# The norm ahead of the feed-forward stages: two products with ones, a root and a reciprocal in place of column sums, a power and transposes

## The chip, the cores and the metric

The kernel runs on one core of a Trainium2 chip. The metric is device time in microseconds (us) of one execution, and lower is better. TensorE (PE) multiplies, VectorE (DVE) and ScalarE (ACT) do elementwise work, GpSimd (POOL) does a little of it, and SyncE (SP) issues most transfers. Each engine has one queue and takes its instructions in the order in which they stand in it.

## The reference

The program is a trunk of two layers over 512 tokens with 1024 features. Each layer mixes tokens by three branches and then runs a gated feed-forward stage with a causal convolution of width 3:

```
for l in range(DEPTH):
    h = rmsnorm(x, norm1_g[l])
    p = h @ w_in[l]
    ...
    x = x + jnp.sum(gates * proj, axis=2) @ w_out[l]
    x = x + conv_ffn(rmsnorm(x, norm2_g[l]), ffn_w_up[l], ffn_conv_w[l], ffn_conv_b[l], ffn_w_down[l])
return rmsnorm(x, final_g)
```

with `rmsnorm(x, g) = x * rsqrt(mean(x*x) + 1e-6) * g`, the mean over the 1024 features of a token. The change is in the second of these norms, `norm2`, once in each layer.

## The kernel before

**Layout.** Activations lie with features on the 128 partitions and tokens along the free axis, so x is eight tiles of 128x512 (names `x`, `xi`). The factor 1/rms of a token is the same for all features. The kernel therefore multiplies by the gain first (`norm_z`), starts the large products on x times gain, and multiplies their results by the token's factor afterwards. That factor, repeated on all 128 partitions, is the tile `rsF` (128x512).

**Exactness.** The products are split in three. Each float32 operand is parted into a rounded `hi` of type fp32r (a ScalarE cast) and a rest `lo` (a VectorE subtraction), and `mm3` issues hi*lo, hi*hi and lo*hi into one PSUM tile (line 153). A weight block of 128x512 comes in by a transfer (`wr`), is cast on ScalarE at line 136 and subtracted on VectorE at line 137. The halves are called `wh`/`wl` or `sh`/`sl`, by the pool that they lie in. One block feeds 12 products.

**The norm.** In `wout` the last eight products of the mixer give the new x. For each, `norm_sq` squares it on ScalarE (line 217) and VectorE adds it to a running tile (line 219), so that one 128x512 tile holds, by token, the sums over the eight blocks. What remains is the sum over the 128 partitions. `norm_stats` makes it by four float32 products with a column of ones, one for 128 tokens, which put the sums of a token on its own partition (128x4, line 229). VectorE scales them and adds epsilon (line 231), and GpSimd raises them to the power -0.5 (line 233, giving `rs`). `norm_rows` turns them back by four transposes of a broadcast column (line 238), and ScalarE copies the result out of PSUM into `rsF` (line 240).

**The feed-forward stage.** `ffn_up` makes 44 output columns of 24 products each. `firstF` runs the first three columns in halves: the first half of each (the four blocks of x that are ready first), and then the second halves. `norm_stats` stands before the fourth of these six steps and `norm_rows` before the fifth. Products that `firstF` issues keep their program order, the others are free to move. A column lies in one of four PSUM tiles `acc` and is released by VectorE's product `fu = acc * rsF` at line 1045. The fifth column takes the tile of the first. Behind `fu` come the convolution (`cv`, lines 1047 to 1049), a tanh on ScalarE (line 1053) and the gating.

**The order.** Apart from the pinned pieces, the order on each engine is set by a scheduler that simulates the program as it is built. An instruction without open inputs may be put anywhere from the place where its buffers are free. Other places that the prediction speaks of: line 456 issues and line 457 casts the small matrices `wua` at a mixer's start, line 472 makes the mixer's first columns `rwc`, line 483 is a tanh on one of them (`wax`), line 528 an exponential, line 960 a Gelu. Lines 970 are two products with the same 128x128 tile of ones in the spatial gating branch.

Of the kernel before, what the change touches and what calls it, by code (L numbers as in the profile page):

```python
# [10 lines left out]
AF = mybir.ActivationFunctionType  # L11
# [5 lines left out]
D = 1024  # L17
# [32 lines left out]
class Emit:  # L50
# [184 lines left out]
    def norm_rows(self):  # L235
# [3 lines left out]
        self.rsF = self.small((128, 512), "rsF", bufs=1)  # L239
        self.nc.scalar.copy(self.rsF, pb)  # L240

    def firstF(self, l, ids, st, at):


        self.h = st["z"]
        pss = [self.acc() for _ in ids]
        gs = [self.matFg(ps, ("wall", l, i, 0), self.h) for ps, i in zip(pss, ids)]
        self.pin = True
        for i, g in enumerate(gs + gs):
            if i == at[0]:  # L250
                self.norm_stats(st)
            if i == at[1]:
                self.norm_rows()
            next(g)
        self.pin = False
        return pss
# [742 lines left out]
    def wout(self, l, mg, xd, st):  # L999
        nc, V = self.nc, self.nc.vector  # L1000
        out = []
        for m in range(8):
            xi = self.u(n="xi")
            nc.sync.dma_start(xi, xd[m])
            ps = self.acc()
            self.matF(ps, ("wall", l, 70 + m, 0), mg)
            V.scalar_tensor_tensor(xi, ps, 0.5, xi, op0=MUL, op1=ADD)
            out.append(xi)
            self.norm_z(st, xi, "n2")
            self.norm_sq(st, xi)  # L1010
        return out
# [15 lines left out]
    def ffn_up(self, l, st, x):  # L1027
        nc, V, A = self.nc, self.nc.vector, self.nc.scalar
        nt = [0]

        def at():
            nt[0] += 1
            return (self.f if nt[0] <= NFP else self.r)(dt=F32R, n="ah")

        act = []
        first = self.firstF(l, (78, 79, 80), st, (3, 4))
        self.xt, turns = {}, [(c, g) for g in range(2) for c in range(NC)]
        for i in range(NFF):
            if l == L - 1 and i % 2 and turns:
                self.turn_x(x, *turns.pop(0))  # L1040
            cs = []
            for j in (i, NFF + i):
                ps = first.pop(0) if first else self.colF(l, 78 + 2 * i + (j >= NFF))
                u = self.u(n="fu")
                V.tensor_tensor(u, ps, self.rsF, op=MUL)  # L1045
                t = self.u(n="cv")
                A.activation(t, u, AF.Identity, scale=self.p("cw2", j), bias=self.p("cb", j))  # L1047
                V.scalar_tensor_tensor(t[:, 1:], u[:, :511], self.p("cw1", j), t[:, 1:], op0=MUL, op1=ADD)  # L1048
                V.scalar_tensor_tensor(t[:, 2:], u[:, :510], self.p("cw0", j), t[:, 2:], op0=MUL, op1=ADD)
                cs.append(t)  # L1050
            g, v = cs
            th = self.u(n="fth")
            A.activation(th, g, AF.Tanh, scale=0.5)
            V.scalar_tensor_tensor(th, th, 1.0, g, op0=ADD, op1=MUL)
            V.tensor_tensor(th, th, v, op=MUL)
            hi, lo = at(), at()
            A.copy(hi, th)
            V.tensor_tensor(lo, th, hi, op=SUB)
            act.append((hi, lo))
        return act  # L1060
# [210 lines left out]
```

## Time and profile before

| what | value |
|---|---|
| median of 3 runs | 1712.36 us (1712.04 to 1712.84) |
| the profiled execution: its time, its span | 1713.67 us, 1710.8 us |
| busy share of PE, DVE, ACT, POOL | 99%, 67%, 44%, 14% |
| granted TensorE clock | 1.000 |

The span runs from the first to the last instruction, and 2.9 us of the profiled execution lie outside it. A matmul of 128x512 is shown with about 0.39 us, but the next one starts before it ends, so that the starts tell the rate. A row of the timeline gives the start, the duration, the engine and the line, and in brackets the idle time before it and what ended that.

### The profile page before, as it was taken

The numbers are of one execution on the slowest core, as the hardware profiler recorded it, in microseconds if no ns is written. First come the engines' busy times: TensorE is split into PE (matmuls) and PEld (weight loads), VectorE is DVE, ScalarE is ACT, GpSimd is POOL, SyncE is SP. The second block draws the span as 40 slices with busy tenths as digits, with TensorE's granted clock in tenths as the row PEclk, the third lists the DMA queues.
The fourth block names the chain that finished last, engine by engine and source line by source line (L and its number), as shares of the span: only waits on it lengthen the run. The fifth ranks groups of instructions, "written<-read, shape, count | busy, mean of one in ns | idle before, by whom it ended". The sixth has DMA issues, their size and how long they took to land.

```text
span 1710.8 us, 27740 instructions
## 1 busy us (share of the span) xinstructions
PE 1700.5 (99%) x10328; PEld 1397.5 (82%) x10328; DVE 1149.7 (67%) x2056; ACT 750.4 (44%) x1258; POOL 247.0 (14%) x328
## 2 busy tenths in 40 slices
PE   9999999999999999999999999999999999999998
PEld 7888877888888888888888888777888888888887
DVE  7887756578568777653367786565775698886432
ACT  6564433534245444343256634345333454443322
POOL 1122235113200000000012203431131000000010
PEclk9999999999999999999999999999999999999999
DMA  5234555535443333233332345555254454432431
GB/s 181 93 104 143 149 140 146 156 116 173 142 154 93 99 99 97 70 116 111 116 113 79 114 143 151 136 145 178 84 188 150 134 135 116 125 110 69 154 99 56
DMA packets 149222, 212.81 MB, mean 124 GB/s; under 512 B 48096, under 2 KB 55264, under 8 KB 149088
## 3 DMA queue, kind: packets, MB, share of 16 engines
q1 hardware_dynamic: 129552, 171.62, 33.5%
q0 software_dynamic: 9600, 21.77, 4.8%
q10 hardware_dynamic: 9936, 17.65, 3.1%
q8 instruction: 81, 1.33, 0.3%
q14 instruction: 53, 0.43, 0.1%
HBM read 182.14 MB, written 23.07 MB: 120 GB/s over the span
## 4 chain that ended last, share of the span: by engine, by line
PE 97%; DMA 1%; DVE 0%; POOL 0%; issue 0%; ACT 0%; SPq 0%; DVEq 0%; POOLq 0%
PE acc L153 86%; PE sm L153 4%; PE sm L634 2%; PE acc L273 1%; PE sm L873 1%; PE sm L548 1%; DMA ws<-sgw 1%; PE sm L978 0%; POOL rs L698 0%; DMA x<-xT 0%; PE sm L511 0%; PE sm L510 0%; PE sm L901 0%; PE sm L928 0%; DVE wl L137 0%
## 5 line engine op out<-in xcount | busy, mean ns | idle before, releaser
L153 PE MATMUL acc<-lo,sh 128*128 128x512 f32 x1108 | 432.2, 391 | 0.0
L153 PE MATMUL acc<-hi,sh 128*128 128x512 f32 x1108 | 431.8, 390 | 0.0
L153 PE MATMUL acc<-hi,sl 128*128 128x512 f32 x1108 | 430.4, 389 | 0.0
L136 ACT CAST sh<-wr 128x512 fp32r<-128x512 f32 (+1 forms) x385 | 236.2, 617 | 409.6 <-PE acc L153 296.4
L137 DVE TENSOR_TENSOR sl<-wr,sh 128x512 fp32r<-128x512 f32 (+1 forms) x385 | 264.6, 691 | 174.9 <-ACT sh L136 106.1
L153 PEld LDWEIGHTS acc<-lo,sh 128*128 128x128 f32 x1108 | 208.0, 188 | 43.7 <-issue 0.3
L153 PEld LDWEIGHTS acc<-hi,sl 128*128 128x128 f32 x1108 | 208.0, 188 | 43.6 <-issue 0.3
L153 PEld LDWEIGHTS acc<-hi,sh 128*128 128x128 f32 x1108 | 208.0, 188 | 43.0 <-issue 0.5
L153 PE MATMUL acc<-lo,wh 128*128 128x512 f32 x556 | 219.5, 395 | 0.0
L136 ACT CAST wh<-wr 128x512 fp32r<-128x512 f32 x194 | 120.5, 621 | 223.7 <-PE acc L153 207.7
L153 PE MATMUL acc<-hi,wl 128*128 128x512 f32 x556 | 217.0, 390 | 0.0
L153 PE MATMUL acc<-hi,wh 128*128 128x512 f32 x556 | 216.6, 390 | 0.0
L137 DVE TENSOR_TENSOR wl<-wr,wh 128x512 fp32r<-128x512 f32 x195 | 137.8, 707 | 104.4 <-ACT wh L136 102.9
L153 PEld LDWEIGHTS acc<-lo,wh 128*128 128x128 f32 x556 | 104.3, 188 | 22.7 <-issue 0.3
L153 PEld LDWEIGHTS acc<-hi,wl 128*128 128x128 f32 x556 | 104.4, 188 | 22.6 <-issue 0.7
L153 PEld LDWEIGHTS acc<-hi,wh 128*128 128x128 f32 x556 | 104.4, 188 | 20.9
L153 PE MATMUL acc<-ah,sh 128*128 128x512 f32 x352 | 108.3, 389 | 0.0
L1045 DVE TENSOR_TENSOR fu<-acc,rsF 128x512 f32<-128x512 f32 x88 | 60.7, 690 | 65.8 <-PE acc L153 65.7
L1047 ACT ACTIVATE cv<-fu,pc 128x512 f32<-128x512 f32 x88 | 71.8, 817 | 47.7 <-DVE fu L1045 44.9
L153 PE MATMUL acc<-wl,hi 128*128 128x512 f32 x192 | 78.3, 408 | 2.1 <-DVE wl L137 2.1
L1048 DVE SCALAR_TENSOR_TENSOR cv<-fu,pc,cv 128x511 f32<-128x511 f32 x88 | 65.7, 747 | 20.2 <-ACT cv L1047 20.1
L153 PEld LDWEIGHTS acc<-ah,sh 128*128 128x128 f32 x352 | 66.1, 188 | 13.6
(320 smaller groups left out, 2434.7 us busy)
## 6 DMA issues: line engine op xcount, KB each, us to landing
wr<-wall SPq DMA_DIRECT2D x480, 256.0 KB, 2.7
gd<-gth ACTq DMA_DIRECT2D x48, 256.0 KB, 2.7
gth<-gd POOLq DMA_DIRECT2D x48, 256.0 KB, 3.5
wr<-wdt SPq DMA_DIRECT2D x44, 256.0 KB, 2.7
wr<-wdn SPq DMA_DIRECT2D x40, 256.0 KB, 2.7
x<-xT SPq DMA_DIRECT2D x8, 256.0 KB, 3.9
tn<-ysq POOLq DMA_DIRECT2D x32, 64.0 KB, 3.6
tab<-rot ACTq DMA_DIRECT2D x8, 256.0 KB, 3.3
```

Source lines behind the costliest of these rows:

```text
L136: self.kept((high or self.nc.scalar.copy)(hi[:, :n], raw[:, :n]))
L137: self.kept(self.nc.vector.tensor_tensor(lo[:, :n], raw[:, :n], hi[:, :n], op=SUB))
L153: i = self.nc.tensor.matmul(*x, **y, **kw)
L273: po(self.nc.tensor.matmul(pss[j], w[:, j * 128:j * 128 + 128], x, start=k == n == 0, stop=k == 7 and n == 2))
L548: i = T.matmul(pK[hv[1 - h], j, :], bk[hv[h], c, 1, :], x[hv[h], c, :], start=True, stop=True)
L634: po(T.matmul(o, l, r, start=start, stop=True, skip_group_check=True))
L873: po(T.matmul(X[h][:, i, :], lhsT, rhs, start=new[h], stop=stop, skip_group_check=True))
L1045: V.tensor_tensor(u, ps, self.rsF, op=MUL)
L1047: A.activation(t, u, AF.Identity, scale=self.p("cw2", j), bias=self.p("cb", j))
L1048: V.scalar_tensor_tensor(t[:, 1:], u[:, :511], self.p("cw1", j), t[:, 1:], op0=MUL, op1=ADD)
```

## The change

In the feed-forward stages, and there alone, `norm_ones` takes the place of `norm_stats` and `norm_rows`. The running tile is split into `hi` and `lo`, two full products with the tile of ones add its partitions, and every partition holds the sums of all 512 tokens at once. ScalarE takes the root of sum/1024 + epsilon out of PSUM, and VectorE takes the reciprocal in place, in two halves of 256. `wout` gets a root of one column of ones in front, whose result nobody reads.

```diff
--- before.py
+++ after.py
@@ -239,6 +239,18 @@
         self.rsF = self.small((128, 512), "rsF", bufs=1)
         self.nc.scalar.copy(self.rsF, pb)
 
+    def norm_ones(self, st):
+
+        hi, lo = self.split(st["acc"])
+        pb = self.sm()
+        for i, x in enumerate((lo, hi)):
+            self.tc.keep_in_program_order(self.nc.tensor.matmul(pb, self.ones, x, start=i == 0, stop=i == 1))
+        self.rsF = self.small((128, 512), "rsF", bufs=1)
+        self.nc.scalar.activation(self.rsF, pb, AF.Sqrt, scale=1.0 / D, bias=self.c("eps"))
+        for i in range(2):
+            h = self.rsF[:, 256 * i:256 * i + 256]
+            self.nc.vector.reciprocal(h, h)
+
     def firstF(self, l, ids, st, at):
 
 
@@ -247,9 +259,11 @@
         gs = [self.matFg(ps, ("wall", l, i, 0), self.h) for ps, i in zip(pss, ids)]
         self.pin = True
         for i, g in enumerate(gs + gs):
-            if i == at[0]:
+            if len(at) == 1 and i == at[0]:
+                self.norm_ones(st)
+            elif i == at[0]:
                 self.norm_stats(st)
-            if i == at[1]:
+            elif i == at[-1]:
                 self.norm_rows()
             next(g)
         self.pin = False
@@ -999,6 +1013,7 @@
     def wout(self, l, mg, xd, st):
         nc, V = self.nc, self.nc.vector
         out = []
+        nc.scalar.activation(self.small((128, 1), "ms"), self.c("ones"), AF.Sqrt)
         for m in range(8):
             xi = self.u(n="xi")
             nc.sync.dma_start(xi, xd[m])
@@ -1033,7 +1048,7 @@
             return (self.f if nt[0] <= NFP else self.r)(dt=F32R, n="ah")
 
         act = []
-        first = self.firstF(l, (78, 79, 80), st, (3, 4))
+        first = self.firstF(l, (78, 79, 80), st, (3,))
         self.xt, turns = {}, [(c, g) for g in range(2) for c in range(NC)]
         for i in range(NFF):
             if l == L - 1 and i % 2 and turns:
```

Line numbers of the kernel after are higher by 14 behind `firstF` and by 15 behind the head of `wout`: line 1060 there is line 1045 here, 1062 is 1047, 1068 is 1053, 497 is 483, 486 is 472, 471 is 457.

**TensorE, start of the first layer's feed-forward stage.** `acc_1095` is the fourth column, the three before it are those of `firstF`. Before, the column sums:

```order
L153 MATMUL acc_1095_5534<-lo_1014_5187,sh_1076_5449 128x512
L153 MATMUL acc_1095_5534<-hi_1013_5186,sh_1076_5449 128x512
L229 MATMUL sm_1072_5438<-con_78,sq_1059_5378 128x1 x4
L153 MATMUL acc_1060_5381<-lo_1025_5234,sh_1064_5386 128x512
L153 MATMUL acc_1060_5381<-hi_1024_5233,sh_1064_5386 128x512
```

and, on TensorE 25 products later, the transposes:

```order
L153 MATMUL acc_1095_5534<-hi_1057_5374,sh_1081_5474 128x512
L153 MATMUL acc_1095_5534<-hi_1057_5374,sl_1082_5475 128x512
L238 MATMUL sm_1078_5465<-con_78,rs_1074_5445 128x128 x4
L153 MATMUL acc_1061_5382<-lo_1025_5234,sh_1067_5404 128x512
L153 MATMUL acc_1061_5382<-hi_1024_5233,sh_1067_5404 128x512
L153 MATMUL acc_1061_5382<-hi_1024_5233,sl_1068_5405 128x512
```

Now both are gone, and the two products stand six products of the fourth column later:

```order
L153 MATMUL acc_1095_5531<-hi_1025_5235,sl_1082_5472 128x512
L153 MATMUL acc_1095_5531<-lo_1037_5283,sh_1081_5471 128x512
L153 MATMUL acc_1095_5531<-hi_1036_5282,sh_1081_5471 128x512
L247 MATMUL sm_1075_5444<-lo_1074_5441,ones_81 128x512
L247 MATMUL sm_1075_5444<-hi_1073_5440,ones_81 128x512
L153 MATMUL acc_1061_5383<-lo_1026_5236,sh_1065_5388 128x512
L153 MATMUL acc_1061_5383<-hi_1025_5235,sh_1065_5388 128x512
L153 MATMUL acc_1061_5383<-hi_1025_5235,sl_1066_5389 128x512
```

The 36 products that are the second halves of the first three columns follow the two in one piece, then the last seven of the fourth column, and then the fifth (`acc_1107`). Nothing else on TensorE has moved in the two layers.

**ScalarE, the same place.** `sq` is the running tile. Before:

```order
L136 CAST sh_1097_5537<-wr_1080_5472 128x512
L136 CAST sh_1100_5555<-wr_1083_5490 128x512
L136 CAST sh_1109_5588<-wr_1096_5535 128x512
L136 CAST sh_1112_5606<-wr_1099_5553 128x512
L136 CAST sh_1118_5631<-wr_1108_5586 128x512
L240 COPY rsF_1079_5470<-sm_1078_5465 128x512
L1047 ACTIVATE cv_1087_5510<-fu_1086_5508,pc_45_181 128x512
L136 CAST sh_1121_5649<-wr_1111_5604 128x512
L1047 ACTIVATE cv_1089_5516<-fu_1088_5514,pc_45_181 128x512
L1053 ACTIVATE fth_1090_5520<-cv_1087_5510 128x512
```

Now:

```order
L145 CAST hi_1073_5440<-sq_1060_5380 128x512
L136 CAST sh_1100_5552<-wr_1083_5487 128x512
L136 CAST sh_1109_5585<-wr_1096_5532 128x512
L249 ACT_TABLE_LOAD
L249 ACTIVATE rsF_1076_5447<-sm_1075_5444,con_78 128x512
L136 CAST sh_1112_5603<-wr_1099_5550 128x512
L136 CAST sh_1118_5628<-wr_1108_5583 128x512
L1062 ACTIVATE cv_1087_5507<-fu_1086_5505,pc_45_181 128x512
L1062 ACTIVATE cv_1089_5513<-fu_1088_5511,pc_45_181 128x512
L136 CAST sh_1121_5646<-wr_1111_5601 128x512
L1068 ACT_TABLE_LOAD
L1068 ACTIVATE fth_1090_5517<-cv_1087_5507 128x512
```

The split stands between two weight casts, the root with a switch of the function table behind the cast `sh_1109`, and one more switch before the first tanh. VectorE has at the same place, before:

```order
L137 TENSOR_TENSOR sl_1101_5556<-wr_1083_5490,sh_1100_5555 128x512
L231 TENSOR_SCALAR ms_1073_5443<-sm_1072_5438 128x4
L137 TENSOR_TENSOR sl_1110_5589<-wr_1096_5535,sh_1109_5588 128x512
L137 TENSOR_TENSOR sl_1113_5607<-wr_1099_5553,sh_1112_5606 128x512
L137 TENSOR_TENSOR sl_1119_5632<-wr_1108_5586,sh_1118_5631 128x512
L1045 TENSOR_TENSOR fu_1086_5508<-acc_1060_5381,rsF_1079_5470 128x512
L1048 SCALAR_TENSOR_TENSOR cv_1087_5510<-fu_1086_5508,pc_45_181,cv_1087_5510 128x511
```

And now VectorE has:

```order
L146 TENSOR_TENSOR lo_1074_5441<-sq_1060_5380,hi_1073_5440 128x512
L137 TENSOR_TENSOR sl_1101_5553<-wr_1083_5487,sh_1100_5552 128x512
L137 TENSOR_TENSOR sl_1110_5586<-wr_1096_5532,sh_1109_5585 128x512
L252 RECIPROCAL rsF_1076_5447<-rsF_1076_5447 128x256 x2
L137 TENSOR_TENSOR sl_1113_5604<-wr_1099_5550,sh_1112_5603 128x512
L1060 TENSOR_TENSOR fu_1086_5505<-acc_1061_5383,rsF_1076_5447 128x512
L1060 TENSOR_TENSOR fu_1088_5511<-acc_1062_5384,rsF_1076_5447 128x512
L137 TENSOR_TENSOR sl_1119_5629<-wr_1108_5583,sh_1118_5628 128x512
L1063 SCALAR_TENSOR_TENSOR cv_1087_5507<-fu_1086_5505,pc_45_181,cv_1087_5507 128x511
```

The two reciprocals stand ahead of one weight subtraction and of the first `fu`.

**ScalarE, start of the first layer.** `wh` are weight casts for the mixer's columns. ScalarE's queue before:

```order
L456 DMA wua_68_234<-wua 128x512
L136 CAST wh_80_329<-wr_77_323 128x512
L457 CAST wus_69_235<-wua_68_234 128x512
L136 CAST wh_85_354<-wr_78_325 128x512
L240 COPY rsF_83_350<-sm_82_345 128x512
L472 ACTIVATE rwc_88_374<-rwp_87_372,omu_60_219 128x512
L472 ACTIVATE rwc_101_400<-rwp_100_398,omu_60_219 128x512
L136 CAST wh_108_416<-wr_79_327 128x512
L472 ACTIVATE rwc_103_405<-rwp_102_403,omu_60_219 128x512
L483 ACTIVATE wax_89_377<-rwc_88_374 64x512 x2
L472 ACTIVATE rwc_105_410<-rwp_104_408,omu_60_219 128x512
L519 ACTIVATE cs_146_562<-rwc_101_400,pc_45_181 128x512
```

Now:

```order
L136 CAST wh_80_329<-wr_77_323 128x512
L1016 ACT_TABLE_LOAD
L1016 ACTIVATE ms_972_5006<-con_78 128x1
L471 CAST wus_69_235<-wua_68_234 128x512
L136 CAST wh_85_354<-wr_78_325 128x512
L240 COPY rsF_83_350<-sm_82_345 128x512
L486 ACTIVATE rwc_88_374<-rwp_87_372,omu_60_219 128x512
L486 ACTIVATE rwc_101_400<-rwp_100_398,omu_60_219 128x512
L136 CAST wh_108_416<-wr_79_327 128x512
L486 ACTIVATE rwc_103_405<-rwp_102_403,omu_60_219 128x512
L497 ACT_TABLE_LOAD
L497 ACTIVATE wax_89_377<-rwc_88_374 64x512 x2
```

The root that is written at the head of `wout` has no inputs that come late, and the scheduler has put it at the layer's start, a whole mixer ahead of `wout`. Behind it the tanh needs a switch back. In the second layer it is the same, where the tanh's switch replaces one that stood at line 528 before. In all the program now has 12 table switches, and before it had 5.

## The prediction

> **What bounds the kernel now.** I read the first part of the page, then the chain that ended last, then the list of TensorE's waits.
>
> ```profile
> span 1710.8 us, 27740 instructions
> PE 1700.5 (99%) x10328; PEld 1397.5 (82%) x10328; DVE 1149.7 (67%) x2056; ACT 750.4 (44%) x1258; POOL 247.0 (14%) x328
> PE 97%; DMA 1%; DVE 0%; POOL 0%; issue 0%; ACT 0%; SPq 0%; DVEq 0%; POOLq 0%
> PE acc L153 <- DVE wl L137: 2.1, 2, 1.1
> PE acc L294 <- DVE rst L291: 1.5, 1, 1.5
> PE acc L273 <- ACT hi L211: 0.4, 1, 0.4
> ```
>
> TensorE is busy for 99% of the span, holds 97% of the chain, and waits for other engines for 2.1 + 1.5 + 0.4 = 4.0 us in all. Only the two waits of 1.1 us or less lie in the middle of the program. So the time is the number of TensorE's instructions by their rate, as long as the others keep up. Two questions follow: what TensorE's own work in the norm costs, and whether the added work on ScalarE and VectorE makes TensorE wait.
>
> **TensorE's part.** The rate comes from the starts in TensorE's timeline around the first layer's norm.
>
> ```profile
> 496.70 0.39 PE L153 MATMUL acc<-lo,sh 128*128 128x512 f32 x1
> ...
> 504.86 0.39 PE L153 MATMUL acc<-lo,sh 128*128 128x512 f32 x1
> 505.09 0.39 PE L153 MATMUL acc<-hi,sh 128*128 128x512 f32 x1
> 505.32 0.95 PE L229 MATMUL sm<-con,sq 128*128 128x1 f32 x8
> ...
> 511.71 0.39 PE L153 MATMUL acc<-hi,sl 128*128 128x512 f32 x1
> 511.93 0.60 PE L238 MATMUL sm<-con,rs 128*128 128x128 f32 x4
> ...
> 517.84 0.39 PE L153 MATMUL acc<-lo,sh 128*128 128x512 f32 x1
> ...
> 1354.27 0.39 PE L153 MATMUL acc<-hi,sh 128*128 128x512 f32 x1
> ...
> 1371.78 0.39 PE L153 MATMUL acc<-lo,sh 128*128 128x512 f32 x1
> ```
>
> From 496.70 to 504.86 there are 36 products by the program's order: 8.16 / 36 = 0.2267 us each. From 504.86 to 511.71 there are 26 with the sums between them: 6.85 - 26 x 0.2267 = 0.96 us for the sums. From 511.71 to 517.84 there are 25 with the transposes between: 6.13 - 25 x 0.2267 = 0.46 us. In the second layer 71 products lie between 1354.27 and 1371.78, with both pieces: 17.51 - 71 x 0.2267 = 1.41 us. So the removed work costs 1.42 and 1.41 us, somewhat less than the 0.95 + 0.60 us of the two rows, whose ends overlap the next product.
>
> The kernel before already has two products like the added ones, in the gating branch:
>
> ```profile
> L970 PE MATMUL sm<-lo,ones x2: 389/389/389, 350.8 to 1200.0; 128*128 128x512 f32 x2
> L970 PE MATMUL sm<-hi,ones x2: 389/389/389, 351.0 to 1200.2; 128*128 128x512 f32 x2
> ```
>
> They have the duration of the products of line 153 and start 0.2 us apart, so each costs 0.227 us: 0.45 us for two. The gain is 1.42 - 0.45 = 0.97 us in the first layer and 0.96 in the second, together 1.93 us. Its bounds: 0 if something else takes it back, 2.83 if the two products were free.
>
> **Is the split there in time?** Rows of VectorE (the last sum into the running tile) and ScalarE (weight casts) in the same stretch:
>
> ```profile
> 500.07 0.69 DVE L219 TENSOR_TENSOR sq<-sq,sq 128x512 f32<-128x512 f32 x1
> 500.12 0.62 ACT L136 CAST sh<-wr 128x512 fp32r<-128x512 f32 x1 [0.23 <-ACT sq L217]
> 502.84 0.62 ACT L136 CAST sh<-wr 128x512 fp32r<-128x512 f32 x1 [2.10 <-PE acc L153]
> 505.56 0.62 ACT L136 CAST sh<-wr 128x512 fp32r<-128x512 f32 x1 [2.10 <-PE acc L153]
> ```
>
> The running tile is complete at 500.76. The cast `hi` (0.62 like its neighbours) fits into the 2.10 us in which ScalarE waits, and `lo` (0.69) follows on VectorE: done at about 502.2. The first product with ones starts seven products after 505.09, at 506.68, 4.5 us later. The split costs nothing; its cover is ScalarE's idle time, and without it TensorE would have to wait only after 4.5 us.
>
> **Is rsF there in time?** This is the piece that could cost something. The products end near 506.90 + 0.39 = 507.29. Then come a table switch, the root and two reciprocals. From ScalarE's timeline at a Gelu, the groups of VectorE's instructions, and its timeline at the first `fu`:
>
> ```profile
> 329.02 0.63 ACT L136 CAST sh<-wr 128x512 fp32r<-128x512 f32 x1
> 329.67 1.28 ACT L960 ACT_TABLE_LOAD   x1
> 330.96 0.63 ACT L960 ACTIVATE sgu<-sgu 128x512 f32<-128x512 f32 x1
> L532 DVE RECIPROCAL F<-cs 128x7 f32<-128x7 f32 x8 | 1.6, 197 | 0.1
> L753 DVE RECIPROCAL TMP<-TMP 128x32 f32<-128x32 f32 x2 | 0.7, 348 | 0.0
> L679 DVE TENSOR_TENSOR S<-S,F 128x256 f32<-128x256 f32 x12 | 5.1, 424 | 0.3
> 513.21 0.68 DVE L1045 TENSOR_TENSOR fu<-acc,rsF 128x512 f32<-128x512 f32 x1
> ```
>
> A switch takes 1.28 us; the root about 0.6, like the other ScalarE passes over 128x512. No reciprocal of 256 columns is shown. The rows of 7 and 32 columns give (348 - 197) / 25 = 6.0 ns for a column, so 348 + 224 x 6.0 = 1.69 us for 256. [...] I take 1.69, from the operation itself. Then: 507.29 + 1.28 + 0.6 = 509.2; two reciprocals, 512.6; one weight subtraction ahead of `fu` in the queue, some 0.6, 513.2; `fu` done at 513.9, the same as before (513.21 + 0.68). The fifth column, which needs that tile, starts 45 products after 506.68, at 516.88 (before: 517.84). The margin is 3.0 us, so this costs nothing as well. The next `fu` follow 0.7 us apart, and each is needed only 24 products, 5.4 us, later. [...]
>
> [...]
>
> **The other switches.** Seven are added, 7 x 1.28 = 9.0 us on ScalarE, which is busy for 44%. Two of them per layer were costed or lie next to it: the root's, above, and the tanh's behind it, where the weight halves are made far ahead (the cast of 505.56 is `sh_1109`, which TensorE first reads 86 products behind the one of 505.09, some 20 us later). The unread root and the switch back lie at the layer's start, for which these are rows of the timelines:
>
> ```profile
> 26.41 0.62 ACT L457 CAST wus<-wua 128x512 fp32r<-128x512 f32 x1 [3.10 <-DMA wua<-wua]
> 31.97 1.26 ACT L483 ACTIVATE wax<-rwc 64x512 f32<-64x512 f32 x2
> 34.50 0.60 ACT L136 CAST wh<-wr 128x512 fp32r<-128x512 f32 x1
> 35.31 0.65 DVE L137 TENSOR_TENSOR wl<-wr,wh 128x512 fp32r<-128x512 f32 x1
> 37.19 0.73 ACT L472 ACTIVATE rwc<-rwp,omu 128x512 f32<-128x512 f32 x1 [1.04 <-DVE rwp L470]
> 38.45 0.39 PE L153 MATMUL acc<-hi,wl 128*128 128x512 f32 x1
> 867.15 0.62 ACT L136 CAST wh<-wr 128x512 fp32r<-128x512 f32 x1 [3.01 <-PE acc L153]
> ```
>
> The unread root (1.28 + about 0.3) falls into idle time of 3.10 us in the first layer and of 3.01 us in the second: nothing. The switch back stands before the tanh of 31.97 and moves the cast of 34.50 and the subtraction of 35.31 by 1.28 us; `wl` is then ready at 37.24, and TensorE first reads it at 38.45. The margin of 2.49 us falls to 1.2. ScalarE's idle 1.04 us at 37.19 takes up most of the delay. Cost nothing. In the second layer a switch at line 528 goes away in return.
>
> Taken out on other engines: line 231, line 233 on GpSimd and ScalarE's copy, none of which TensorE waits for. The sum for the profiled execution is 1713.67 - 1.93 = 1711.7 us. The median is 1.31 us lower than that execution, so 1712.36 - 1.93 = 1710.4 us.
>
> **Rivals.**
>
> *The gain is given back (1712.4).* If somewhere behind the norms another engine sets the pace, TensorE arrives there earlier and waits. For it: the two waits for `wl` show such places. Against: 4.0 us of waits in all, and what VectorE does there is itself released by TensorE's products. Both gains would be lost.
>
> *More is gained (1708.3).* If the two waits for `wl`, 2.1 us, also go because ScalarE and VectorE are loaded otherwise: 1710.4 - 2.1. For it: the second layer loses a switch at line 528 ahead of the second wait. Against: it gets one earlier in return, and the order there hasn't moved.
>
> [...]
>
> *A late start of the mixer (slower: 1715.9).* If the two ScalarE pieces at a layer's start (1.28 + 1.28 + 0.2) weren't absorbed and came back in full as waits for `wl` in each layer: 1710.4 + 2 x 2.76. Against: the idle rows just shown.
>
> That the change doesn't do what it says is excluded by the order: the products, root and reciprocals stand there.
>
> **How the numbers follow.** Chances: forecast 0.72, given back 0.11, more gained 0.06, rsF late 0.06, late mixer 0.05. The time is 1710.4. The forecast's own range is 1709.5 to 1711.3 (runs of before lie 0.8 apart). Up to 1713.2 the given-back case and part of a late rsF are in, down to 1709.0 a part of the larger gain: 1709.0 to 1713.2 holds some 0.85. A measurement of this kernel can tell about 0.2%, 3.4 us, from no change: below 1708.9 it is faster, above 1715.8 slower. The larger gain lies beyond the first bound, and half of the last rival beyond the second, with something for what I haven't seen: 0.06 faster, 0.89 same, 0.05 slower.
>
> **What would show it.** Right: two products at the new line 247 with 0.45 us between their neighbours, no wait of TensorE at 507 or for the fifth column's tile, `fu` near 513, twelve table loads of 1.28 us, and the weight subtraction of 35.31 up to 1.3 us later. Wrong: reciprocals above 3 us, a wait of TensorE behind `fu`, or waits for `wl` at a layer's start or longer ones than 1.1 us.

## The result, and the profile after

The changed kernel takes 1709.25 us (median of 15 runs, 1708.48 to 1710.52), beside 1712.36 us for the kernel before (15 runs, 1711.23 to 1713.84). The ratio is 0.9982, with a 95% interval from 0.9975 to 0.9989, so between 1.9 and 4.3 us are gained. The forecast was 1.93 us. The profiled execution took 1709.09 us, with a span of 1707.4 us.

From the page of the changed kernel, its span, busy times and the shares of the chain that ended last:

```profile
span 1707.4 us, 27709 instructions
PE 1697.3 (99%) x10308; PEld 1395.7 (82%) x10308; DVE 1156.7 (68%) x2060; ACT 758.1 (44%) x1269; POOL 244.2 (14%) x326
PE 98%; DMA 1%; DVE 0%; POOL 0%; issue 0%; ACT 0%; SPq 0%; DVEq 0%; POOLq 0%
```

And the list of TensorE's waits (total, times, longest, in us):

```profile
PE acc L153 <- DVE wl L137: 1.7, 2, 0.9
PE acc L308 <- DVE rst L305: 1.5, 1, 1.5
PE acc L287 <- DVE wh L136: 0.8, 1, 0.8
```

Nothing has changed in kind. TensorE is still busy for 99% and waits at the same three lines of the program, 4.0 us in all as before. It waits nowhere for `rsF` or `fu`. It has 20 instructions fewer: in each layer the sums had 8 and the transposes 4, and the products with ones are 2. With the reciprocals VectorE's busy time is higher by 7.0 us in all, and with the table loads ScalarE's by 7.7, beside TensorE's work.

TensorE's timeline of the changed kernel at the first layer's norm, and at the first product of the fifth column:

```profile
505.90 0.39 PE L153 MATMUL acc<-hi,sh 128*128 128x512 f32 x1
506.13 0.39 PE L247 MATMUL sm<-lo,ones 128*128 128x512 f32 x1
506.36 0.39 PE L247 MATMUL sm<-hi,ones 128*128 128x512 f32 x1
506.58 0.39 PE L153 MATMUL acc<-lo,sh 128*128 128x512 f32 x1
...
516.33 0.39 PE L153 MATMUL acc<-lo,sh 128*128 128x512 f32 x1
```

The two products with ones stand in the stream like any other: 506.58 - 506.13 = 0.45 us for both, and no idle time in brackets at any row, the fifth column's included. Now the chain from the sums to `fu`, first ScalarE's timeline, then VectorE's:

```profile
500.15 0.62 ACT L145 CAST hi<-sq 128x512 fp32r<-128x512 f32 x1
...
505.66 1.28 ACT L249 ACT_TABLE_LOAD   x1
506.95 0.69 ACT L249 ACTIVATE rsF<-sm,con 128x512 f32<-128x512 f32 x1
```

```profile
500.84 0.68 DVE L146 TENSOR_TENSOR lo<-sq,hi 128x512 fp32r<-128x512 f32 x1
...
507.67 3.37 DVE L252 RECIPROCAL rsF<-rsF 128x256 f32<-128x256 f32 x2 [1.31 <-ACT rsF L249]
510.95 0.63 DVE L137 TENSOR_TENSOR sl<-wr,sh 128x512 fp32r<-128x512 f32 x1
511.50 1.42 DVE L1060 TENSOR_TENSOR fu<-acc,rsF 128x512 f32<-128x512 f32 x2
```

The split is done at 501.52, and its first reader starts at 506.13. The table load begins at 505.66, while TensorE still makes the sums, and ends at 506.94, 0.2 us behind the last of them (506.36 + 0.39). So it is all but out of the chain. The row of 511.50 holds two `fu`; the first ends near 512.2, and the fifth column needs it at 516.33. The margin is 4.1 us.

### The profile page after: what moved, and what is told of

It reads as the page before. It is cut to its first block, busy times and chain, and to the rows that moved or that the text cites. A ratio compares the mean times of both kernels' runs of the same rounds, so it can differ in the third digit from the quotient of the medians.

```text
span 1707.4 us, 27709 instructions
## 1 busy us (share of the span) xinstructions
PE 1697.3 (99%) x10308; PEld 1395.7 (82%) x10308; DVE 1156.7 (68%) x2060; ACT 758.1 (44%) x1269; POOL 244.2 (14%) x326
## 4 chain that ended last, share of the span: by engine, by line
PE 98%; DMA 1%; DVE 0%; POOL 0%; issue 0%; ACT 0%; SPq 0%; DVEq 0%; POOLq 0%
PE acc L153 87%; PE sm L153 4%; PE sm L648 2%; PE acc L287 1%; PE sm L887 1%; PE sm L562 1%; DMA ws<-sgw 1%; PE sm L992 0%; POOL rs L712 0%; DMA g<-pcols 0%; PE sm L525 0%; PE sm L524 0%; PE sm L915 0%; PE sm L942 0%; PE sm L800 0%
```

## The experiments

**Where the time went.** Four points of TensorE's timeline part the program into stretches that hold one thing each: the gating branch's products with ones in both layers, the first sums of the second layer's `norm1`, and the last product. The rows of the kernel before, and of the changed one:

```profile
350.81 0.39 PE L970 MATMUL sm<-lo,ones 128*128 128x512 f32 x1
...
863.50 0.95 PE L229 MATMUL sm<-con,sq 128*128 128x1 f32 x8
...
1199.99 0.39 PE L970 MATMUL sm<-lo,ones 128*128 128x512 f32 x1
...
1704.29 0.40 PE L153 MATMUL acc<-sh,ah 128*128 128x256 f32 x2
```

```profile
350.26 0.39 PE L984 MATMUL sm<-lo,ones 128*128 128x512 f32 x1
...
861.77 0.95 PE L229 MATMUL sm<-con,sq 128*128 128x1 f32 x8
...
1197.58 0.39 PE L984 MATMUL sm<-lo,ones 128*128 128x512 f32 x1
...
1700.91 0.40 PE L153 MATMUL acc<-sh,ah 128*128 128x256 f32 x2
```

Stretch A runs to the first point and C from the second to the third: each holds a mixer and no changed norm. B lies between them, and D runs from the third point to the end of the last product: each holds one changed norm and its feed-forward stage. The starts give, for all kernels of the study (us):

| kernel | A | B | C | D |
|---|---|---|---|---|
| before | 350.81 | 512.69 | 336.49 | 504.70 |
| before, another execution | 350.07 | 512.68 | 336.35 | 504.70 |
| before, with the unread root | 350.04 | 512.47 | 335.81 | 504.71 |
| changed | 350.26 | 511.51 | 335.81 | 503.73 |
| changed, another execution | 350.75 | 511.51 | 335.27 | 503.74 |
| changed, without the unread root | 350.24 | 511.51 | 336.36 | 503.74 |
| both norms | 351.03 | 512.93 | 336.53 | 505.16 |
| ten times the products | 349.92 | 515.62 | 336.15 | 507.82 |
| three times the reciprocals | 350.02 | 517.41 | 336.06 | 509.58 |
| `ws` first | 349.07 | 511.51 | 334.64 | 503.74 |

In two executions of one kernel B and D repeat to 0.01 us; A and C scatter by a microsecond, whichever norm the kernel has. That makes two questions. Do B and D fall by what TensorE's instructions cost, or by another cause (the switches, a change in how the engines meet)? And what makes A and C scatter, which the gain beyond 1.93 us must come from?

**The same kernel again**, timed beside the next two on one chip.

> The changed kernel once more. Theory P (TensorE's own work alone): two stages of 0.97 us less, so 1.93 us below the kernel before, a ratio of 0.9989; what came out beyond it, 3.1 - 1.9 = 1.2 us, is scatter between executions, and the starts in a second trace differ from the first by up to about 1 us at places that have nothing to do with the norms. Rival S (the table switches also help the rest of the program): 3.1 us again, 0.9982, and the steps of the shift against the kernel before lie at the same places as in the first trace.

Measured: 1709.05 us (11 runs), with 1711.67 for the kernel before; the ratio is 0.9986, from 0.9977 to 0.9994. D differs from the kernel before by 504.70 - 503.74 = 0.96 us, and B by 1.18. The gain in the medians is 2.6 us here and 3.1 in the first comparison, and isn't better known than to about a microsecond.

> The kernel before once more, one look, for its trace: how far TensorE's starts differ between two executions of one kernel. Theory P: up to about 1 us over the span, gathered in small steps where TensorE runs many short products or waits for a weight half. Rival S: less than 0.3 us, so that 1.4 us of shift outside the norms must be an effect.

Measured: one execution of 1711.59 us, with a span of 1709.9. Its B and D are those of the first trace, its A is 0.74 us shorter, and so is TensorE's one wait for `wl` in that stretch, 0.23 us by 0.97.

**Switches, one way and the other.** First the changed kernel without the unread root in `wout`, and so with 8 table loads in place of 12:

```diff
-        nc.scalar.activation(self.small((128, 1), "ms"), self.c("ones"), AF.Sqrt)
```

> The changed kernel without the unread root at the head of wout. On every engine the same instructions in the same order, but for eight ScalarE instructions less: two roots and two table loads in front of the mixers, two loads back (less one that returns at the exponential). Theory P: ScalarE's idle time hid them, so the time is that of the changed kernel within 0.3 us (ratio to the kernel before 0.9989). Rival S: the 1.2 us beyond the forecast came from the moved switches and go with them: 1.2 us slower than the changed kernel. Rival L (the late mixer of the prediction in small): the switches cost and the time falls by up to 2.8 us more.

Measured: 1709.44 us (11 runs), ratio 0.9987 from 0.9978 to 0.9996; B and D are as with the root to 0.01 us. Then the kernel before with that line added, and so with 8 table loads in place of 5:

> The kernel before with the unread root alone; the sums, the power and the transposes stay. Eight table loads in place of five. Theory P: 1.0000, the kernel before within 0.3 us, and the weight subtraction of 35.31 is 1.3 us later with TensorE's starts unmoved. Rival S: 1.2 us faster, 0.9993. Rival L: slower by up to 5.5 us.

Measured: 1711.36 us (11 runs), ratio 0.9999 from 0.9990 to 1.0008. Whatever would put a gain or a loss down to the switches falls on both sides: the four further loads there and the three here cost nothing that can be measured, and bring nothing. The unread root in particular doesn't spare the load at the norm. The groups of ScalarE's instructions in the changed kernel show why:

```profile
L1016 ACT ACT_TABLE_LOAD x2 | 2.6, 1283 | 0.0
L497 ACT ACT_TABLE_LOAD x2 | 2.6, 1283 | 0.0
L974 ACT ACT_TABLE_LOAD x2 | 2.6, 1283 | 0.0
L249 ACT ACT_TABLE_LOAD x2 | 2.6, 1283 | 0.0
```

The root's set comes in at line 1016 at the layer's start, the tanh's at line 497 and the Gelu's at line 974 follow, and so the load at line 249 is still there, twice. What hides the pieces at a layer's start is seen in ScalarE's timeline:

```profile
23.39 1.28 ACT L1016 ACT_TABLE_LOAD   x1
24.68 0.20 ACT L1016 ACTIVATE ms<-con 128x1 f32<-128x1 f32 x1
26.43 0.62 ACT L471 CAST wus<-wua 128x512 fp32r<-128x512 f32 x1 [1.55 <-DMA wua<-wua]
...
32.10 1.28 ACT L497 ACT_TABLE_LOAD   x1
...
35.94 0.60 ACT L136 CAST wh<-wr 128x512 fp32r<-128x512 f32 x1
...
38.63 0.72 ACT L486 ACTIVATE rwc<-rwp,omu 128x512 f32<-128x512 f32 x1 [1.04 <-DVE rwp L484]
```

The first load and the root lie in the idle time before the cast of `wus`, of which 1.55 us are left from 3.10. The second moves the weight cast from 34.50 to 35.94, and TensorE doesn't wait for it.

**The removed work back in.** The changed kernel with the old sums, power and transposes at their old places beside the new norm. Their result isn't used, one column of it is copied and left (the edit in part):

```diff
+                self.norm_stats(st)
...
+            elif len(at) == 1 and i == at[0] + 1:
+                self.norm_rows(False)
```

> The changed kernel with the old column sums, the power and the four transposes of each feed-forward stage put back beside the new ones; of their result one column is copied and nobody reads it. Theory P: TensorE gets back what the prediction priced at 1.42 and 1.41 us, so the time is 2.8 us above the changed kernel: 1.6 us or so below 1713.6 on a scale on which the changed kernel stands at 1709.1, that is 1711.9, and level with the kernel before (ratio 1.000 to 1.001). In the trace the stretch from the first layer's norm to the next mixer's norm grows from 355.64 to 357.06 us, the one from the second norm to the end from 347.87 to 349.28. Rival D (what was saved were the durations of the records, 0.95 + 0.60): 3.1 us. Rival H (the sums were hidden): no change against the changed kernel, 0.9985.

Measured: 1712.51 us (11 runs), ratio to the kernel before 1.0003 from 0.9994 to 1.0012. B grows by 512.93 - 511.51 = 1.42 us and D by 505.16 - 503.74 = 1.42. That is the price that the prediction read from the spacing of starts (1.42 and 1.41), not that of the durations shown in the rows (0.95 + 0.60 = 1.55), and it isn't hidden.

**The added work ten times.** Each pair of products with ones is made ten times into the same tile:

```diff
-        for i, x in enumerate((lo, hi)):
-            self.tc.keep_in_program_order(self.nc.tensor.matmul(pb, self.ones, x, start=i == 0, stop=i == 1))
+        for i, x in enumerate((lo, hi) * 10):
+            self.tc.keep_in_program_order(self.nc.tensor.matmul(pb, self.ones, x, start=i % 2 == 0, stop=i % 2 == 1))
```

> The changed kernel with the two products with ones issued ten times in each stage, the last pair being used: 18 more products in each, the order on the other engines the same. Theory P: 18 x 0.2267 = 4.08 us in each stage, 8.16 us in all, 1717.3 where the changed kernel stands at 1709.1; one pair then costs 0.453 us. Rival: the products cost their whole duration of 0.39 us, 14.0 us in all; or nothing, if TensorE has slack there.

Measured: 1718.03 us (6 runs), ratio 1.0034 from 1.0022 to 1.0047. B is 4.11 us longer than in the changed kernel and D 4.08; 18 products by 0.2267 us are 4.08. With this, both sides of TensorE's sum are measured: 1.42 out, 0.45 in.

**The reciprocals late.** Each half is inverted three times, which gives the same value, and 6.9 us more on VectorE ahead of `fu`:

```diff
-        for i in range(2):
+        for i in (0, 1) * 3:
```

> The changed kernel with the reciprocals taken three times over (the reciprocal of the reciprocal of the reciprocal, so the value is the same): four more of 256 columns in each stage, 4 x 1.66 = 6.6 us more on VectorE ahead of the first product with rsF, with three weight subtractions between and behind them, where the changed kernel has one. In the trace of the changed kernel that product ends at 512.2, and the fifth column needs its tile at 516.3: a margin of 4.2 us. Theory P (rsF costs nothing until the fifth column needs the tile, and one for one from there): about 6.6 + 1.2 + some 0.6 of waiting for the casts = 8.4 us later, less 4.2, so TensorE stands for about 4.2 us in each stage, 8.5 us in all: 1717.6. By the margin of 3.0 us of the prediction it would be 2.4 us more. Rival H: VectorE's queue is covered further on too, and the time stays at 1709.1.

Measured: 1721.24 us (5 runs), ratio 1.0055 from 1.0043 to 1.0068. The pause came about as reckoned, and something else with it. TensorE's waits for `fu` in the list of its waits, and then its timeline around the first one:

```profile
PE acc L153 <- DVE fu L1060: 7.9, 2, 4.0
```

```profile
515.86 0.39 PE L153 MATMUL acc<-hi,sl 128*128 128x512 f32 x1
520.21 0.50 PE L153 MATMUL acc<-lo,sh 128*128 128x512 f32 x1 [3.96 <-DVE fu L1060]
...
521.03 0.62 PE L153 MATMUL acc<-lo,sh 128*128 128x512 f32 x1
521.45 0.63 PE L153 MATMUL acc<-hi,sh 128*128 128x512 f32 x1
...
524.43 0.40 PE L153 MATMUL acc<-hi,sl 128*128 128x512 f32 x1
524.67 0.39 PE L153 MATMUL acc<-lo,sh 128*128 128x512 f32 x1
```

Behind the pause of 3.96 us the products start 0.42 us apart for 3.4 us, from 521.03 to 524.43, instead of 0.23. B is longer than in the changed kernel by 5.90 us and D by 5.85, so each layer pays 1.9 us beyond the pause. The windows of the same kernel name it (the stretch and its length, the busy times of the five engines with their instructions, TensorE's granted clock, the DMA engines' share and GB/s):

```profile
520.20:524.50 4.30, 4.29 (x12) 3.38 (x13) 3.93 (x6) 2.78 (x3) 0.00 (x0) 0.60 0.32 116
524.50:529.00 4.50, 4.50 (x21) 3.70 (x20) 3.81 (x7) 3.72 (x7) 0.00 (x0) 1.00 0.05 8
```

The clock is 0.60 in the mean of the first window and 1.00 behind it. To tell whether the extra goes with the length of the pause (theory P) or is a fixed price from some length on (theory G), three kernels make it shorter and longer, by further reciprocals that leave the values as they are. The edit of the shortest is shown; the second has 192 in place of 128, and the longest has `(0, 1, 0, 1, 0, 1, 0, 0)` in the first loop and not the second one:

```diff
-        for i in range(2):
+        for i in (0, 1, 0, 0):
...
+        for w in (128, 128):
+            self.nc.vector.reciprocal(self.rsF[:, 0:w], self.rsF[:, 0:w])
```

> The changed kernel with two further reciprocals over 256 columns and two over 128 (the first half is inverted five times, the second once, so the values are the same). With 1.72 us for 256 columns and 0.87 for 128, and the stall of 3.96 us that four further ones of 256 columns made, TensorE's pause behind fu should be 3.96 - 2 x 1.72 + 2 x 0.87 = 2.3 us in each layer. Theory G (a pause longer than some length between 1.1 and 4.0 us lowers the clock for a fixed time): either no product slower, and a span of 1707.4 + 2 x 2.3 = 1712.0, or the same extra of 1.9 us in each layer, 1715.8. [...] Rival P (the extra grows with the pause, 1.9 / 3.96 = 0.48 of it): products spaced wider for about 1.1 us in sum in each layer, a span of 1714.2.

> As the one with the pause of 2.3 us, with 192 columns in place of 128 (1.3 us each by the same rate): a pause of 3.96 - 2 x 1.72 + 2 x 1.3 = 3.1 us in each layer. Theory G: no product slower, a span of 1707.4 + 2 x 3.1 = 1713.6, or the same extra of 1.9 us in each layer, 1717.4, or the extra in one layer alone, if the length from which it acts is near 3 us. Rival P: an extra of 0.48 x 3.1 = 1.5 us in each layer, a span of 1716.6.

> The changed kernel with six further reciprocals of 256 columns (the first half five times, the second three times, the same values): a pause of 3.96 + 2 x 1.72 = 7.4 us in each layer. Theory G: the extra behind the pause is the same 1.9 us, a span of 1707.4 + 2 x (7.4 + 1.9) = 1726.0. Rival P: an extra of 3.5 us in each layer, 1729.2.

Measured, one execution each, beside 1712.3 us for the kernel before; B and D are given against the changed kernel's 511.51 and 503.73:

| kernel | time, span | pause | B | D | beyond the pause |
|---|---|---|---|---|---|
| two of 128 | 1717.32, 1715.6 | 2.84 | +4.77 | +3.14 | 1.93 and 0.30 |
| two of 192 | 1720.22, 1718.5 | 3.4 | +5.35 | +5.32 | 1.9 |
| three times | 1721.24, 1719.2 | 3.96 | +5.90 | +5.85 | 1.9 |
| six more | 1729.09, 1727.4 | 7.5 | +9.38 | +9.39 | 1.8 |

The pauses of the first two came out 0.3 to 0.5 us longer than expected, in part since 128 columns take 0.94 us and 192 take 1.34. Theory P falls: from 3.4 to 7.5 us the extra stays at 1.8 to 1.9. The first kernel holds the decisive pair, in TensorE's timeline, and in the windows behind its two pauses:

```profile
519.37 0.50 PE L153 MATMUL acc<-lo,sh 128*128 128x512 f32 x1 [2.84 <-DVE fu L1062]
...
1371.73 0.50 PE L153 MATMUL acc<-lo,sh 128*128 128x512 f32 x1 [2.84 <-DVE fu L1062]
```

```profile
519.37:523.40 4.03, 4.03 (x11) 3.21 (x12) 3.74 (x6) 1.50 (x2) 0.00 (x0) 0.59 0.09 33
1371.73:1376.00 4.27, 4.27 (x19) 3.53 (x20) 3.98 (x9) 2.75 (x3) 0.00 (x0) 1.00 0.09 33
```

The same pause in the same place lowers the clock in the first layer and not in the second, with the same share of the DMA engines (0.09) in both windows. So the slow spell isn't contention with transfers. The waits of up to 1.42 us that the kernels of the table have in their mixers don't bring it: behind the longest of them the products start 0.33 us apart once and then 0.23 to 0.24. Two narrower windows show where it lies in the first layer:

```profile
519.37:520.13 0.76, 0.76 (x3) 0.67 (x4) 0.54 (x1) 0.76 (x2) 0.00 (x0) 1.00 0.46 175
520.13:523.54 3.41, 3.41 (x9) 2.64 (x8) 3.34 (x5) 0.74 (x2) 0.00 (x0) 0.50 0.00 0
```

The clock is 1.00 for 0.76 us behind the pause and then 0.50 for 3.41 us, in which nothing is transferred. So the spell doesn't begin with the pause's end here, nor does it with three times the reciprocals, where the first wide spacing follows the start at 521.03, 0.82 us behind the pause. Behind the first pause of 7.5 us the spacing is wide from the first product on (starts at 525.08, 525.67 and 526.10). By the two pauses of 2.84 us it isn't the length of a pause alone that decides. What else does isn't shown: no run moved a pause to try it.

**What scatters in A and C.** In the mixers TensorE waits for `wl`, between 0.23 and 1.08 us in stretch A and between 0.29 and 1.42 in C in the nine rows of the table that have these waits. What is late there? From the timelines of the kernel before, TensorE's and then VectorE's:

```profile
307.84 0.39 PE L153 MATMUL acc<-wh,lo 128*128 128x512 f32 x1
309.20 0.50 PE L153 MATMUL acc<-wl,hi 128*128 128x512 f32 x1 [0.97 <-DVE wl L137]
309.53 0.40 PE L153 MATMUL acc<-wh,hi 128*128 128x512 f32 x1
```

```profile
302.72 0.70 DVE L366 TENSOR_TENSOR ws<-ws,con 128x512 f32<-128x512 f32 x1 [3.19 <-DMA ws<-sgw]
...
307.85 0.69 DVE L699 TENSOR_TENSOR y<-y,rs 128x512 f32<-128x512 f32 x1 [0.81 <-POOL rs L698]
308.46 0.68 DVE L137 TENSOR_TENSOR wl<-wr,wh 128x512 fp32r<-128x512 f32 x1
```

VectorE stands at 302.72 for 3.19 us, because the gating branch's matrix `ws` hasn't landed, and everything behind it in VectorE's queue is late with it, the subtraction for `wl` last. The theory of the late `ws`: issue its transfer ahead of two others on SyncE's queue, and both waits go. This is the changed kernel without the unread root, and with

```diff
         with self.tc.high_priority():
+            self.nc.sync.dma_start(self.ws, self.a["sgw"][l])
             self.nc.sync.dma_start(self.gup, self.a["gup"][l])
...
-        self.nc.sync.dma_start(self.ws, self.a["sgw"][l])
```

> The changed kernel without the unread root, and with the transfer of the spatial gating matrix (ws) issued ahead of two other small ones, since in the traces VectorE stands for about 3 us in front of its mask product, the weight subtractions behind it come late, and TensorE waits for one of them, 0.2 to 1.1 us, near 309 and near 1156. Theory W: these two waits are the only ones in the middle of the program and go away, 1.2 to 1.7 us on the average: 1707.9 where the kernel without the root stands at 1709.4, and the scatter of the stretches between the norms falls below 0.3 us. Rival G: the wait is set by GpSimd's power (1.7 to 2.3 us) in the same chain, and only its part before the power moves: less than 0.5 us. Rival N: the waits move to another place.

Measured: 1707.22 us (6 runs, 1706.73 to 1707.79), ratio to the kernel before 0.9972 from 0.9960 to 0.9983. TensorE's waits that are left, and in VectorE's timeline the same instruction:

```profile
PE acc L308 <- DVE rst L305: 1.5, 1, 1.5
PE acc L287 <- ACT hi L211: 0.3, 1, 0.3
```

```profile
299.75 0.69 DVE L380 TENSOR_TENSOR ws<-ws,con 128x512 f32<-128x512 f32 x1 [1.42 <-DMA ws<-sgw]
```

Both waits for `wl` are gone. The instruction comes 3.0 us earlier, A is 1.17 us shorter than without the moved transfer and C 1.72, and B and D are the same to 0.01. The theory holds for the waits, and this version is the fastest of the study: its slowest run, 1707.79, lies below the fastest of every other kernel.

The gain is larger than the 1.2 to 1.7 us expected. One reason is that a wait costs more than the idle time in its brackets: from 307.84 to 309.53 there are two products, so 1.69 - 2 x 0.2267 = 1.24 us are lost for 0.97. In the kernel without the root the same working gives 1.04 us for a wait of 0.77 and 1.23 for one of 0.96, together 2.27 of the 2.89 us in A and C. The rest lies elsewhere in A and C and isn't explained. The waits aren't all of the scatter either. Without the bracketed time the nine rows still lie 1.0 us apart in A, where they lay 1.1 apart with it, and 0.45 apart in C, where it was 1.26. So the waits for `wl` make most of C's scatter and little of A's, whose cause stays open. Whether the scatter falls below 0.3 us, as theory W has it, can't be told from one trace.

## Why the prediction was right, and where it wasn't

**TensorE's part held.** The forecast gain of 0.97 + 0.96 us is D's 0.97 and, against the kernel before with the unread root, B's 512.47 - 511.51 = 0.96. Against the kernel before itself B falls by 1.18, of which 0.21 us lie far behind the norm, as is said below. Putting the old work back costs 1.42 in each layer, where 1.42 and 1.41 were forecast, and the added products cost 0.227 each. The rival that gives the gain back falls: the feed-forward stages keep it in full.

**The split** cost nothing, as forecast: it was done 4.6 us ahead of its reader, where 4.5 was reckoned.

**`rsF` was in time, with a margin of 4.1 us in place of 3.0.** The reciprocal, whose duration no row had shown, took 1.72 us by 1.69 forecast, so the slope of the 7 and 32 columns carries to 256. Too late was the step that puts the table switch behind the sums: it ran beside them and ended 0.2 us behind the last one, so 1.1 of its 1.28 us fell out of the chain. The root took 0.69 by 0.6. The whole switch, from the end of the cast before the load (505.64) to the start of the root (506.95), took 1.31 us.

A late `rsF`, to which the prediction gives a chance of 0.06 and a part of the range up to 1713.2, didn't come: no run shows a switch or a single reciprocal of 256 columns long enough for it (1.28 and at most 1.75 us). What it costs is shown by the kernels with further reciprocals: TensorE then stands at the fifth column, in each layer, and pays more than the pause, 0.30 us more behind the one pause of 2.84 us without a slow spell and 1.8 to 1.9 in the other cases. Between 1.5 and 2.8 us no pause was measured.

**The other switches were hidden**, as forecast: the weight cast at the layer's start moved by 1.44 us, where 1.28 was reckoned, and no wait came of it. The late-mixer rival falls.

**The time: 1709.25 by 1710.4 forecast.** The measured time lies 0.25 us below the forecast's own range of 1709.5 to 1711.3, and within the wider one, which ends at 1709.0. The terms of the sum that belong to the norms were right; the rest isn't shown to be an effect of theirs, and that it stayed inside the wider range is luck. In the profiled pair the gain is 3.38 us: A gives 0.55, B 1.18, C 0.68 and D 0.97. Of B's, 0.21 us appear in both traces of the kernel before and in no other; they lie near 744 us, far behind the norm. There a product starts at 744.14, right behind the subtraction that makes its `sl` (743.40 + 0.69), and that one is late in VectorE's queue behind a ScalarE cast at 736.42, for whose weight block ScalarE stood 3.64 us. Why the block lands later in this kernel is open. A and C together are 685.9 to 687.6 us in the four traces with the old norm's work (686.8 in the mean) and 686.0 to 687.3 in eight with the new norm alone, the three with pauses of 2.84 to 7.5 us among them (686.4): what could be the norm's in it, 0.4 us, is less than the scatter. The step that was off is thus the last one: 1.93 us were subtracted from a median of three runs as if nothing else moved between the medians of two kernels. The kernel before had a median of 1712.36 again in 15 runs, and of 1711.67 and 1712.0 in the later comparisons. That scatter comes in part from the waits for `wl`. The rival "more is gained" named these very waits, but the changed norms don't remove them (1.7 us were left of 2.1), while an earlier `ws` does, for 2.3 of the 2.9 us by which A and C are shorter.

## What to carry to other kernels

Where one engine is busy for 99%, price an edit by the spacing of starts around it and not by the rows' durations; 1.42 against 1.55 us was told apart here by putting the removed work back. Look at a long wait of a helper engine (3.19 us for `ws`) even when the bounding engine waits only a little behind it: one transfer moved ahead brought about as much as both norms, 2.3 us at the two waits by 1.93 in the two feed-forward stages. And a stall cost somewhat more than its length here even when it was short, 0.27 us at waits of 0.77 to 0.97 us; check the granted clock behind it before pricing a longer one.

## What the runs showed that was not expected

**A pause of TensorE can cost 1.8 to 1.9 us more than its length.** Behind pauses of 3.4, 3.96 and 7.5 us, in both layers, and behind one of two pauses of 2.84 us, products started 0.42 to 0.43 us apart for about 3.4 us, with a granted clock of 0.59 and 0.60 in the two windows shown that take in some of the time behind it, and of 0.50 in the narrower one. The price is 1.8 to 1.9 us beyond the pause, and 0.30 without the slow spell. By an estimate from these numbers that adds up: in 3.41 us at 0.427 us a product instead of 0.2267, 3.41 x (1 - 0.2267 / 0.427) = 1.6 us are lost, and 0.30 came with the pause that had no slow spell. Behind waits of about 1 us the spacing was 0.33 once and then 0.23 to 0.24. A pause of 2.84 us was enough for the slow spell in the first layer and not in the second; what makes the difference isn't shown.

**The table load didn't wait for the data of its activation.** The load at line 249 ran from 505.66 to 506.94 in the first layer and from 1352.97 to 1354.25 in the second. The second product of the sums that its root reads started at 506.36 and at 1353.67.

**An instruction without late inputs goes where the scheduler has room.** The root that stands at the head of `wout` ran at 24.68 us, a mixer ahead of it, with two other sets loaded in between. So it spared no load, and the four loads that it brings per program cost nothing that can be measured, with ScalarE busy for 44%.
